# Between two layers: memory products ahead of the transition, and row scaling on VectorE with plain transposes in place of fp32 products with a diagonal

## The chip, the cores and the metric

The kernel runs on one core of a Trainium2 chip. TensorE (PE in the rows, PEld for its weight loads), VectorE (DVE), ScalarE (ACT) and GpSimd (POOL) each run their own queue of instructions in order and wait for each other by semaphores; SyncE (SP) issues the loads from HBM. The metric is the time of one execution on the device in microseconds (us), lower is better.

## The reference, cut to what matters

Two layers run one after the other on 256 tokens of 1024 channels. The first ends in a mixture of experts and a norm with a weight; the second starts with a norm of that result and multiplies it by a wide weight matrix. Beside it, a second input, the memory, is normed and multiplied by its own weights; it depends on nothing of the first layer.

```
x = x + g2 * hier_moe(...)                       # end of the first layer
x = rms_norm(x) * final_norm_w                   # its output
h = rms_norm_2(x, g_mix); proj = h @ w_in        # start of the second
kv_m = rms_norm_2(mem, g_mem) @ w_mem_kv         # (256 x 1024) @ (1024 x 1280)
k_m = rms_norm_2(kv_m[keys], g_k_mem); v_m = kv_m[values]
```

## The kernel before

The 256 tokens stand as two halves of 128 rows. Activations that are multiplied by weights stand transposed, as eight k-tiles of 128 channels by 256 tokens. A float32 product is made of three cheaper ones: each factor is split into a rounded part, hi, and the rest, lo, and the products hi by hi, lo by hi and hi by lo are summed in PSUM. For weights, ScalarE rounds (`whi`, L111) and either GpSimd (L113) or VectorE (L115) subtracts (`wlo`). `unit` makes such a pair for one k-tile of up to 512 columns; four pairs of buffers rotate. Its counter `nunit` with `lo_pool` says who subtracts: every `lo_pool`-th time it is GpSimd. `mm_tok` (L187 to L189) then makes six products per k-tile: hi and lo of the activations with `whi`, and hi with `wlo`, for each half.

`transition` joins the layers. From the four PSUM tiles `moe` it makes w = moe times the norm weight (`tw`, L1207), sums of squares on ScalarE and VectorE, and from them, in some sixteen small VectorE instructions on 128 x 4 values (L1212 to L1218 and `rsqrt`, L126 to L135), two factors per row. One gives the residual `x2` (L1235), the other the second layer's normed input. For that one the kernel makes two 128 x 128 diagonals of the factors, `dm` (`tdm`, L1222), and multiplies each 128 x 128 block of w by its diagonal in float32 (L1229), which scales the rows and transposes them at once. The results are split into `h_hi` on ScalarE (L1114) and `h_lo` on VectorE (L1115), with the gain `g_mix`.

`mem_kv` multiplies the memory (`mh`, `ml`) by its weights in three groups: m = 0, 256 columns of keys, and m = 1 and 2, 512 columns of values each, eight k-tiles per group. In it `lo_pool` is 1, so that GpSimd makes every `wlo`. After the groups the keys are normed (`head_norm_T`: another small VectorE chain, on 128 x 8 values) and transposed (L1161).

`phase_c` is the second layer; its first products take the k-tiles of `h_hi` and `h_lo` against 320 columns of w_in (`tok(320)`). Later stages load 512 columns (2 MB) at a time into three ring buffers, each of which is given back once its k-tiles have been split.

The order of the instructions on each engine is made by a scheduler as the program is built; only SyncE's order is written by hand. Written order counts through `run`: both generators are started, `mem_kv` up to a yield within m = 1, then the rest of `transition`, then the rest of `mem_kv`. `tc.issue_after(i)` puts the instructions that are written in its block behind instruction i on i's engine. Transposes and products of the transition write PSUM tiles of one pool of four banks, which groups m = 0, 1 and 2 use too.

Of the kernel before, what the change touches and what calls it, by code (L numbers as in the profile page):

```python
# [8 lines left out]
F32 = mybir.dt.float32  # L9
# [3 lines left out]
OP = mybir.AluOpType  # L13
# [3 lines left out]
D = 1024  # L17
# [29 lines left out]
class Loader:  # L47
# [31 lines left out]
    def next(self):  # L79
        return self.ready.popleft()[0]  # L80
# [10 lines left out]
class Kern:  # L91
# [1072 lines left out]
    def mem_kv(self, sb, wk):  # L1164
        nc, ld = self.nc, self.ld
        kt = sb.tile([128, 1024], F32, tag="I", name="kmt")[:, 0:512].rearrange("p (t n) -> p t n", t=2)
        self.lo_pool = 1
        for m in range(3):
            w = 512 if m else 256
            p = self.pst2("mm", w)  # L1170
            ch = ld.next()
            v = self.chunk(ch, 8, w)
            for j in range(2):
                k = slice(j * 4, j * 4 + 4)
                self.mm_tok(p, v[:, k], 0, w, self.mh[:, k], self.ml[:, k], start=j == 0, stop=j == 1)
                if m == 1 and j == 0:
                    yield
            ld.give(ch)
            for t in range(2):
                o = self.vm[:, t, 512 * m - 512:512 * m] if m else kt[:, t]  # L1180
                nc.scalar.activation(o, p[t], AF.Copy)
        self.lo_pool = 4
        self.head_norm_T(wk, self.kmT, kt, self.row("g_k_mem"))
# [13 lines left out]
    def transition(self, sb, wk):  # L1197

        nc = self.nc
        jk = sb.tile([128, 2, 512], F32, tag="ck", name="tjk")  # L1200
        jk = [jk[:, 0], jk[:, 1]]
        w = sb.tile([128, 2, D], F32, tag="A", name="tw")
        ss = wk.tile([128, 2, 2, 2], F32, name="tss")
        for h in range(2):
            for t in range(2):
                r = slice(h * 512, h * 512 + 512)
                nc.vector.tensor_tensor(out=w[:, t, r], in0=self.moe[t][h], in1=self.fw[:, r], op=OP.mult)  # L1207
                self.square_sum(jk[0], self.moe[t][h], ss[:, 0, t, h:h + 1])
                sq = self.square_sum if h else self.square_sum_v
                sq(jk[1 - h], w[:, t, r], ss[:, 1, t, h:h + 1])  # L1210
        s = wk.tile([128, 2, 2], F32, name="ts")
        nc.vector.tensor_tensor(out=s, in0=ss[:, :, :, 0], in1=ss[:, :, :, 1], op=OP.add)  # L1212

        v = wk.tile([128, 4], F32, name="tv")
        nc.vector.tensor_scalar(v[:, 0:2], s[:, 0], 1.0 / D, EPS, op0=OP.mult, op1=OP.add)
        e = wk.tile([128, 2], F32, name="te")
        nc.vector.tensor_scalar(e, v[:, 0:2], EPS, None, op0=OP.mult)
        nc.vector.scalar_tensor_tensor(v[:, 2:4], s[:, 1], 1.0 / D, e, op0=OP.mult, op1=OP.add)  # L1218
        r = self.rsqrt(wk, v, 4)
        dm = sb.tile([128, 2048], F32, tag="E", name="tdm")[:, 0:256].rearrange("p (t n) -> p t n", t=2)  # L1220
        for t in range(2):
            nc.vector.tensor_scalar(dm[:, t], self.ident, r[:, 2 + t:3 + t], None, op0=OP.mult)  # L1222
        yield
        for j in range(4):
            p = self.pst("aux")
            for i in range(2):
                for t in range(2):
                    k = 2 * j + i
                    nc.tensor.matmul(p[:, i * 256 + t * 128:i * 256 + t * 128 + 128],  # L1229
                                     w[:, t, k * 128:k * 128 + 128], dm[:, t], start=True, stop=True)  # L1230
            for i in range(2):
                k = 2 * j + i
                self.split_scaled(self.hh[:, k], self.hl[:, k], p[:, i * 256:i * 256 + 256], self.col("g_mix", k))
        for t in range(2):
            nc.vector.tensor_scalar(self.x2[:, t], w[:, t], r[:, t:t + 1], None, op0=OP.mult)  # L1235
# [573 lines left out]
    def run(self, ctx):  # L1809
        nc, tc, a = self.nc, self.tc, self.a  # L1810
# [41 lines left out]
        p = self.xbctx.enter_context(tc.tile_pool(name="r3p", bufs=1))  # L1852
# [3 lines left out]
        with ExitStack() as c:  # L1856
# [15 lines left out]
            sb = cc.enter_context(tc.tile_pool(name="pc", bufs=1, reuse_waits="tile"))  # L1872
# [5 lines left out]
            tr, mk = self.transition(sb, wk), self.mem_kv(sb, wk)  # L1878
            next(tr)
            next(mk)  # L1880
            for part in (tr, mk):
                for _ in part:
                    pass
        self.neg = sb.tile([128, 384], F32, name="neg")
        nc.gpsimd.memset(self.neg, 0.0)
        for o in (0, 256):
# [129 lines left out]
```

## Time and profile before

| what | value |
|---|---|
| median of three runs | 1151.42 us (1149.34 to 1154.03) |
| the profiled execution's own time | 1148.48 us |
| its span, first to last instruction | 1146.8 us |
| TensorE busy | 1058.3 us, 92% of the span |
| VectorE / ScalarE / GpSimd busy | 548.2 / 437.2 / 198.2 us |
| granted TensorE clock, mean | 0.981 |

The times of the rows are microseconds from the span's start. In timeline rows the columns are start, duration, engine, line and operation, output and inputs, shape, and in square brackets how long the engine had been idle and what ended that. A duration runs from start to result; instructions of one engine overlap, so that the pitch between starts is shorter.

### The profile page before, as it was taken

The numbers are of one execution on the slowest core, as the hardware profiler recorded it, in microseconds if no ns is written. First come the engines' busy times: TensorE is split into PE (matmuls) and PEld (weight loads), VectorE is DVE, ScalarE is ACT, GpSimd is POOL, SyncE is SP. The second block draws the span as 40 slices with busy tenths as digits, with TensorE's granted clock in tenths as the row PEclk, the third lists the DMA queues.
The fourth block names the chain that finished last, engine by engine and source line by source line (L and its number), as shares of the span: only waits on it lengthen the run. The fifth ranks groups of instructions, "written<-read, shape, count | busy, mean of one in ns | idle before, by whom it ended". The sixth has DMA issues, their size and how long they took to land.

```text
span 1146.8 us, 18483 instructions
## 1 busy us (share of the span) xinstructions
PE 1058.3 (92%) x6937; PEld 716.6 (62%) x6937; DVE 548.2 (48%) x1345; ACT 437.2 (38%) x982; POOL 198.2 (17%) x189
## 2 busy tenths in 40 slices
PE   4989998999979998987889989998999999999998
PEld 2767777534333431321233678887898888998997
DVE  4498656312121310201221558475796776664664
ACT  3444433211111210101011646565774555655653
POOL 1453112000000000000010732221121132222221
PEclk9999989999989999999999989999999999999999
DMA  9885668599989999999999633552632233554531
GB/s 370 335 349 232 259 260 350 197 421 409 421 336 421 420 417 420 421 422 420 421 421 418 255 141 145 215 184 77 221 108 99 90 148 147 220 185 183 220 147 38
DMA packets 36281, 314.40 MB, mean 274 GB/s; under 512 B 4160, under 2 KB 4672, under 8 KB 5328
## 3 DMA queue, kind: packets, MB, share of 16 engines
q1 hardware_dynamic: 36176, 313.05, 68.1%
q8 instruction: 59, 0.97, 0.3%
q14 instruction: 46, 0.38, 0.1%
HBM read 324.57 MB, written 1.05 MB: 284 GB/s over the span
## 4 chain that ended last, share of the span: by engine, by line
PE 48%; DMA 17%; DVE 4%; ACT 1%; issue 1%; POOL 0%; DVEq 0%; SPq 0%; ACTq 0%
DMA xb<-w 12%; DMA ring<-w 5%; PE mm L176 5%; PE mm L175 5%; PE mm L174 5%; PE pb L937 5%; PE mm L189 4%; PE mm L187 4%; PE mm L188 4%; PE pb L977 3%; PE ff L187 3%; PE ff L188 3%; PE ff L189 3%; PE pb L910 1%; PE aux L1555 1%
## 5 line engine op out<-in xcount | busy, mean ns | idle before, releaser
L111 ACT ACTIVATE whi<-ring 128x512 fp32r<-128x512 f32 (+3 forms) x378 | 228.6, 613 | 196.8 <-PE mm L175 92.6
L113 POOL TENSOR_TENSOR wlo<-ring,whi 128x512 fp32r<-128x512 f32 (+2 forms) x124 | 160.6, 1303 | 499.4 <-ACT whi L111 472.4
L115 DVE TENSOR_TENSOR wlo<-ring,whi 128x512 fp32r<-128x512 f32 (+2 forms) x254 | 177.9, 704 | 139.9 <-ACT whi L111 126.4
L937 PE MATMUL pb<-xb,xT 128*32 128x512 f32 x736 | 134.3, 595 | 9.2 <-DMA xb<-w 9.2
L937 PE MATMUL pb<-ring,xT 128*32 128x512 f32 x672 | 122.5, 595 | 7.0 <-DMA ring<-w 7.0
L963 DVE SCALAR_TENSOR_TENSOR g<-g,pb 128x256 f32<-128x256 f32 x22 | 9.3, 421 | 193.2 <-ACT g L962 193.2
L937 PEld LDWEIGHTS pb<-xb,xT 128*32 128x32 f32 x736 | 34.1, 109 | 87.5 <-issue 60.6
L962 ACT ACTIVATE g<-pb 128x256 f32<-128x256 f32 x22 | 8.4, 383 | 198.2 <-PE pb L937 192.8
L977 PE MATMUL pb<-xb,hT 128*32 128x512 f32 x464 | 79.9, 602 | 2.3 <-DMA xb<-w 1.8
L937 PEld LDWEIGHTS pb<-ring,xT 128*32 128x32 f32 x672 | 30.6, 109 | 72.3 <-issue 51.8
L175 PE MATMUL mm<-h_lo,whi 128*128 128x256 f32 (+1 forms) x264 | 75.3, 285 | 0.0
L176 PE MATMUL mm<-h_hi,wlo 128*128 128x256 f32 (+1 forms) x264 | 75.3, 286 | 0.0
L174 PE MATMUL mm<-h_hi,whi 128*128 128x256 f32 (+1 forms) x264 | 75.2, 285 | 0.0
L113 POOL TENSOR_TENSOR ml<-ring,mh 128x256 fp32r<-128x256 f32 x8 | 5.6, 733 | 400.3 <-DMA xb<-w 400.3
L175 PE MATMUL mm<-xg_lo,whi 128*128 128x256 f32 x256 | 71.2, 280 | 0.0
L174 PE MATMUL mm<-xg_hi,whi 128*128 128x256 f32 x256 | 70.7, 280 | 0.6 <-DVE xg_lo L1115 0.6
L176 PE MATMUL mm<-xg_hi,wlo 128*128 128x256 f32 x256 | 70.9, 279 | 0.0
L187 PE MATMUL mm<-whi,h_hi 128*128 128x512 f32 (+2 forms) x144 | 54.4, 379 | 0.1
L188 PE MATMUL mm<-whi,h_lo 128*128 128x512 f32 (+2 forms) x144 | 53.8, 376 | 0.0
L984 DVE SCALAR_TENSOR_TENSOR Y<-pb,gs,g2row 128x512 f32<-128x512 f32 x22 | 16.5, 750 | 78.0 <-PE pb L977 77.1
L189 PE MATMUL mm<-wlo,h_hi 128*128 128x512 f32 (+2 forms) x144 | 45.6, 379 | 6.1 <-issue 3.8
L176 PEld LDWEIGHTS mm<-h_hi,wlo 128*128 128x128 f32 (+1 forms) x264 | 49.6, 188 | 1.4 <-issue 1.0
(530 smaller groups left out, 2219.5 us busy)
## 6 DMA issues: line engine op xcount, KB each, us to landing
xb<-w SPq DMA_DIRECT2D x110, 1024.0 KB, 15.5
ring<-w SPq DMA_DIRECT2D x82, 1024.0 KB, 13.4
ring<-w_in SPq DMA_DIRECT2D x18, 2048.0 KB, 7.5
ring<-w_ada SPq DMA_DIRECT2D x12, 2048.0 KB, 14.1
ring<-w_up SPq DMA_DIRECT2D x8, 2048.0 KB, 7.3
ring<-w_down SPq DMA_DIRECT2D x8, 2048.0 KB
ring<-w_out SPq DMA_DIRECT2D x2, 2048.0 KB, 11.8
ring<-w_mem_kv SPq DMA_DIRECT2D x2, 2048.0 KB
```

Source lines behind the costliest of these rows:

```text
L111: self.nc.scalar.activation(hi, src, AF.Copy)
L113: self.nc.gpsimd.tensor_tensor(out=lo, in0=src, in1=hi.bitcast(F32), op=OP.subtract)
L115: self.nc.vector.tensor_tensor(out=lo, in0=src, in1=hi.bitcast(F32), op=OP.subtract)
L174: nc.tensor.matmul(out, hv[:, k], xh[:, k0 + k], start=f, stop=False)
L175: nc.tensor.matmul(out, hv[:, k], xl[:, k0 + k], start=False, stop=False)
L176: nc.tensor.matmul(out, lv[:, k], xh[:, k0 + k], start=False, stop=l)
L187: nc.tensor.matmul(out[t], xh[:, k, s], hv[:, 0], start=f, stop=False)
L188: nc.tensor.matmul(out[t], xl[:, k, s], hv[:, 0], start=False, stop=False)
L189: self.last = nc.tensor.matmul(out[t], xh[:, k, s], lv[:, 0], start=False, stop=l)
L937: nc.tensor.matmul(q[r, :], x[:, k, r], w[side[i]][:, h * 512:h * 512 + 512], start=k == 0, stop=k == KT - 1)
L977: nc.tensor.matmul(y[h][r, :], hT[:, f * 128 + i * 32:f * 128 + i * 32 + 32], w[side[i]][:, h * 512:h * 512 + 512], start=f == 0, stop=f == 3)
L984: nc.vector.scalar_tensor_tensor(Y, y[h], gs, self.g2row[:, h * 512:h * 512 + 512], op0=OP.mult, op1=OP.mult)
```

## The change

It does four things. The yield of `mem_kv` moves from the middle of m = 1 to the middle of m = 2, so that when the rest of `transition` is written, all but four k-tiles of the memory's products have been written. The rest of `transition` is put behind the last of those products on TensorE. From m = 1 on `lo_pool` is 2 instead of 1: every other `wlo` of m = 1 and m = 2 is VectorE's. And the diagonals with their float32 products go: VectorE scales the rows of w by the factor in four pieces of 128 x 512 (`ws`, shown as `tws`), and TensorE transposes the sixteen blocks of 128 x 128.

```diff
@@ mem_kv
         for m in range(3):
+            if m:
+                self.lo_pool = 2
...
                 self.mm_tok(p, v[:, k], 0, w, self.mh[:, k], self.ml[:, k], start=j == 0, stop=j == 1)
-                if m == 1 and j == 0:
+                if m == 2 and j == 0:
                     yield
@@ transition
-        dm = sb.tile([128, 2048], F32, tag="E", name="tdm")[:, 0:256].rearrange("p (t n) -> p t n", t=2)
-        for t in range(2):
-            nc.vector.tensor_scalar(dm[:, t], self.ident, r[:, 2 + t:3 + t], None, op0=OP.mult)
+        ws = sb.tile([128, 2, D], F32, tag="E", name="tws")
+        for h in range(2):
+            for t in range(2):
+                c = slice(h * 512, h * 512 + 512)
+                nc.vector.tensor_scalar(ws[:, t, c], w[:, t, c], r[:, 2 + t:3 + t], None, op0=OP.mult)
         yield
...
-                    nc.tensor.matmul(p[:, i * 256 + t * 128:i * 256 + t * 128 + 128],
-                                     w[:, t, k * 128:k * 128 + 128], dm[:, t], start=True, stop=True)
+                    nc.tensor.transpose(p[:, i * 256 + t * 128:i * 256 + t * 128 + 128],
+                                        ws[:, t, k * 128:k * 128 + 128], self.ident)
@@ run
-            for part in (tr, mk):
-                for _ in part:
+            with tc.issue_after(self.last.ins):
+                for _ in tr:
                     pass
+            for _ in mk:
+                pass
```

What this does to the order on TensorE: before, the sixteen products with the diagonals stand behind the last k-tile of m = 1 and in front of all eight of m = 2 (`mm_13574` and `mm_13575` are m = 1, `mm_13697` is m = 2).

```order
L189 MATMUL mm_13574<-wlo_13685,mh 128x512
L189 MATMUL mm_13575<-wlo_13685,mh 128x512
L1229 MATMUL aux_13616<-tdm,tw 128x128
L1229 MATMUL aux_13625<-tdm,tw 128x128
L1229 MATMUL aux_13616<-tdm,tw 128x128 x3
L1229 MATMUL aux_13625<-tdm,tw 128x128 x3
L1229 MATMUL aux_13634<-tdm,tw 128x128 x4
L1229 MATMUL aux_13643<-tdm,tw 128x128 x4
L187 MATMUL mm_13697<-whi_13699,mh 128x512
```

These sixteen (32 instructions) are gone from this place.

After, the first eight transposes stand behind the fourth k-tile of m = 2 (`whi_13693`; the groups' tiles are now `mm_13661` and `mm_13662`), and its last four k-tiles behind them.

```order
L188 MATMUL mm_13662<-whi_13693,ml 128x512
L189 MATMUL mm_13661<-wlo_13694,mh 128x512
L189 MATMUL mm_13662<-wlo_13694,mh 128x512
L1233 MATMUL aux_13703<-ident,tws 128x128 x4
L1233 MATMUL aux_13712<-ident,tws 128x128 x4
L187 MATMUL mm_13661<-whi_13741,mh 128x512
L188 MATMUL mm_13661<-whi_13741,ml 128x512
```

The other eight stand behind all of m = 2 and the first four products of the second layer (`mm_13841`, `mm_13842`).

```order
L187 MATMUL mm_13842<-whi_13843,h_hi 128x320
L188 MATMUL mm_13842<-whi_13843,h_lo 128x320
L1233 MATMUL aux_13721<-ident,tws 128x128 x4
L1233 MATMUL aux_13730<-ident,tws 128x128 x4
L189 MATMUL mm_13841<-wlo_13844,h_hi 128x320
```

On VectorE, before, the end of the transition's small chain stands alone: the last step of `rsqrt`, the diagonals, the residual, and then the first step for the memory's keys.

```order
L133 TENSOR_TENSOR rqt_13475<-rqy_13471 128x4
L134 TENSOR_TENSOR rqt_13475<-rqt_13475,rqw_13473 128x4
L135 SCALAR_TENSOR_TENSOR rqy_13471<-rqt_13475,rqy_13471 128x4
L1222 TENSOR_SCALAR tdm<-ident,rqy_13471 128x128 x2
L1235 TENSOR_SCALAR x_13436<-tw,rqy_13471 128x1024 x2
L120 TENSOR_SCALAR rqv_13792<-hnss_13782 128x8
```

After, two `wlo` stand within that chain (of the seventh k-tile of m = 1, and, here the first row, of the first of m = 2), five steps for the keys lie among its last ones, and the `wlo` of the third k-tile of m = 2 (`wlo_13684`) stands behind the four scalings and half of the residual.

```order
L115 TENSOR_TENSOR wlo_13664<-ring_64,whi_13663 128x512
L133 TENSOR_TENSOR rqt_13475<-rqy_13471 128x4
L134 TENSOR_TENSOR rqt_13475<-rqt_13475,rqw_13473 128x4
L135 SCALAR_TENSOR_TENSOR rqy_13471<-rqt_13475,rqy_13471 128x4
L120 TENSOR_SCALAR rqv_13794<-hnss_13784 128x8
L133 TENSOR_TENSOR rqt_13475<-rqy_13471 128x4
L126 TENSOR_SCALAR rqi_13796<-rqv_13794 128x8
L130 TENSOR_SCALAR rqw_13800<-rqv_13794 128x8
L134 TENSOR_TENSOR rqt_13475<-rqt_13475,rqw_13473 128x4
L128 TENSOR_SCALAR rqy_13798<-rqi_13796 128x8
L135 SCALAR_TENSOR_TENSOR rqy_13471<-rqt_13475,rqy_13471 128x4
L133 TENSOR_TENSOR rqt_13802<-rqy_13798 128x8
```

The steps for the keys are new there. Further on the same queue, where the diagonals and the residual stood, are now the scalings, with a `wlo` between the halves of the residual.

```order
L1226 TENSOR_SCALAR tws<-tw,rqy_13471 128x512 x4
L1239 TENSOR_SCALAR x_13436<-tw,rqy_13471 128x1024
L115 TENSOR_TENSOR wlo_13684<-ring_64,whi_13683 128x512
L1239 TENSOR_SCALAR x_13436<-tw,rqy_13471 128x1024
L134 TENSOR_TENSOR rqt_13802<-rqt_13802,rqw_13800 128x8
```

So the scalings stand behind more of VectorE's queue than the diagonals did, and the `wlo` of a product on TensorE stands behind the scalings. On ScalarE two roundings stand between the third and the last of the transition's square sums instead of three; on GpSimd eight of the sixteen subtractions of m = 1 and m = 2 are gone; SyncE's order is the same.

## Rows read from the trace of the kernel before

**Rows 1.** The page's first line: the span.

```profile
span 1146.8 us, 18483 instructions
```

**Rows 2.** Stretches: length, busy time per engine (count), granted clock, DMA share, GB/s.

```profile
647.00:658.50 11.50, 10.54 (x47) 8.25 (x45) 5.57 (x8) 9.90 (x35) 11.50 (x10) 1.00 0.36 125
658.50:663.80 5.30, 0.00 (x0) 0.00 (x0) 4.95 (x13) 1.24 (x3) 3.35 (x3) 0.90 0.87 354
663.80:670.10 6.30, 6.28 (x31) 6.28 (x32) 3.95 (x15) 2.07 (x5) 0.00 (x0) 0.54 0.01 3
670.10:1146.80 476.70, 465.50 (x2890) 412.38 (x2888) 309.74 (x725) 277.73 (x632) 107.78 (x84) 1.00 0.41 151
```

**Rows 3.** Timeline of TensorE around the products with the diagonals.

```profile
656.98 0.39 PE L187 MATMUL mm<-whi,mh 128*128 128x512 f32 x1
...
657.88 0.61 PE L189 MATMUL mm<-wlo,mh 128*128 128x512 f32 x2
663.82 1.01 PE L1229 MATMUL aux<-tdm,tw 128*128 128x128 f32 x3 [5.32 <-DVE tdm L1222]
...
670.16 0.47 PE L187 MATMUL mm<-whi,mh 128*128 128x512 f32 x1
```

**Rows 4.** Instructions on the diagonals' tile: min/median/max in ns, first and last start.

```profile
L1229 PE MATMUL aux<-tdm,tw x32: 275/421/579, 663.8 to 670.1; 128*128 128x128 f32 x32
```

**Rows 5.** Timeline of VectorE, the transition's small chain.

```profile
652.86 0.36 DVE L1212 TENSOR_TENSOR ts<-tss 128x4 f32<-128x4 f32 x1 [5.80 <-ACT tjk L1107]
653.25 1.22 DVE L1215 TENSOR_SCALAR tv<-ts 128x2 f32<-128x2 f32 x1
...
660.69 1.18 DVE L133 TENSOR_TENSOR rqt<-rqy 128x4 f32<-128x4 f32 x1
661.90 0.16 DVE L134 TENSOR_TENSOR rqt<-rqt,rqw 128x4 f32<-128x4 f32 x1
...
663.48 0.48 DVE L1222 TENSOR_SCALAR tdm<-ident,rqy 128x128 f32<-128x128 f32 x2
663.87 1.41 DVE L1235 TENSOR_SCALAR x<-tw,rqy 128x1024 f32<-128x1024 f32 x2
```

**Rows 6.** Timeline of GpSimd over the same time.

```profile
646.44 15.41 POOL L113 TENSOR_TENSOR wlo<-ring,whi 128x512 fp32r<-128x512 f32 x12
```

**Rows 7.** Timeline of VectorE later: two square sums of one shape.

```profile
689.94 1.35 DVE L1110 SCALAR_TENSOR_TENSOR jv<-ck 128x256 f32<-128x256 f32 x1 [0.83 <-ACT ck L1284]
...
691.67 0.42 DVE L1110 SCALAR_TENSOR_TENSOR jv<-ck 128x256 f32<-128x256 f32 x1
```

**Rows 8.** Timeline of GpSimd over the first of these.

```profile
689.72 1.30 POOL L113 TENSOR_TENSOR wlo<-ring,whi 128x512 fp32r<-128x512 f32 x1 [3.12 <-ACT whi L111]
```

**Rows 9.** Groups by shape, 640 to 672 us: count, busy, mean ns, idle before.

```profile
L111 ACT ACTIVATE whi<-ring 128x512 fp32r<-128x512 f32 x12 | 7.4, 628 | 2.3 <-PE mm L188 1.6 <-issue 0.5 <-POOL wlo L113 0.2
...
L189 PE MATMUL mm<-wlo,mh 128*128 128x512 f32 x18 | 5.8, 396 | 1.0 <-POOL wlo L113 1.0
...
L1115 DVE SCALAR_TENSOR_TENSOR h_lo<-aux,pk,h_hi 128x256 fp32r<-128x256 f32 x8 | 3.8, 482 | 2.4 <-ACT h_hi L1114 2.3
...
L1114 ACT ACTIVATE h_hi<-aux,pk 128x256 fp32r<-128x256 f32 x8 | 3.5, 471 | 8.7 <-PE aux L1229 8.5 <-DVE h_lo L1115 0.2
```

**Rows 10.** Groups by shape over the whole span: VectorE's subtraction.

```profile
L115 DVE TENSOR_TENSOR wlo<-ring,whi 128x512 fp32r<-128x512 f32 x236 | 169.5, 721 | 130.5 <-ACT whi L111 122.4 <-PE mm L189 4.7 <-DVEq L1465 2.4
```

**Rows 11.** Timeline of TensorE later: ten plain transposes and what follows them.

```profile
829.92 1.25 PE L1192 MATMUL aux<-ident,qn 128*128 128x128 f32 x10
830.92 0.36 PE L174 MATMUL mm<-h_hi,whi 128*128 128x256 f32 x1
```

**Rows 12.** Timeline of SyncE: loads of w_in.

```profile
679.74 7.21 SPq L104 DMA_DIRECT2D ring<-w_in  x2
```

**Rows 13.** Timeline of TensorE: the first product with the second chunk.

```profile
705.14 0.40 PE L187 MATMUL mm<-whi,h_hi 128*128 128x512 f32 x1
```

**Rows 14.** Timeline of TensorE: its longest wait for VectorE in the second layer.

```profile
711.34 0.73 PE L189 MATMUL mm<-wlo,h_hi 128*128 128x512 f32 x2 [2.23 <-DVE wlo L115]
```

## The prediction

> **What bounds the kernel now.** The change touches one place, so the stretch between the layers was read first, by windows [rows 2]. From 647.0 to 658.5 us TensorE is busy for 10.54 of 11.50 us. Then it does nothing for 5.3 us while DVE works for 4.95, and for the next 6.3 us it is busy at a granted clock of 0.54, about the lower of its two levels, 1.2 GHz. From 670.1 to the end it is busy for 465.50 of 476.70 us, and the DMA engines for 0.41 of it: behind this place TensorE sets the time, and what it wins here should reach the end.
>
> The timeline of TensorE says what the two pieces are [rows 3]. The last product of m = 1 ends at 657.88 + 0.61 = 658.49. The idle 5.32 us after it end on DVE's `tdm`, the diagonals; then come the 32 records of the products with diagonals [rows 4], and the first product of m = 2 starts at 670.16. So 670.16 − 658.49 = 11.67 us lie between two groups that depend on nothing of the first layer: 5.32 of waiting and 6.35 of products.
>
> The timelines of DVE and GpSimd say why `tdm` is late [rows 5, 6]. DVE's chain of sixteen small instructions starts with `ts` at 652.86 (released by ScalarE's last square sum) and reaches `tdm` at 663.48. While GpSimd subtracts without a gap, twelve in 15.41 us (1.28 each) from 646.44 to 661.85, a DVE instruction on four columns takes 1.2 us, one for each GpSimd instruction; from 661.90 on eight of them fit into 663.48 − 661.90 = 1.58 us, 0.198 each. Some 7 us of the chain's 10.6 are thus waiting for GpSimd.
>
> **The change part by part.** *Removed:* the whole 11.67 us from TensorE's order, if what fills the hole is ready in time.
>
> *Transposes added.* Ten plain transposes run from 829.92 to the next product at 830.92, 0.10 us each [rows 11]; sixteen are **+1.6 us**. At the lower clock they could be twice that, 3.2; I take 1.6, as work runs up to them and the clock was 1.00 while it did [rows 2].
>
> *Moved: when the scalings must be ready.* Four products of 512 columns start between 656.98 and 657.88, 0.225 us each, and a k-tile has six: 1.35 us [rows 3]. With four k-tiles of m = 2 put in, the first transpose is due at 658.49 + 4 × 1.35 = 663.89.
>
> *When they are ready.* `ts` starts when ScalarE ends its last square sum; one rounding fewer stands ahead of it, 0.63 us [rows 9], of which I take 0.55. DVE's work from there, without GpSimd's hindrance: sixteen steps of 0.198 = 3.16; two subtractions of 0.72 [rows 10] = 1.44; five steps for the keys, 0.99; four scalings of 128 x 512. For these the near rows are two `tdm` of 128 columns in 0.48 and two halves of `x` of 1024 in 1.41 [rows 5], 0.24 and 0.70 each, between them 0.44; four are 1.75. Together 7.34.
>
> GpSimd, which now makes every other `wlo`, runs one of 1.28 us for each two k-tiles (2.7 us), three or four while the chain runs. Each may hold DVE for between 0 and 1.28 us, so 0 to 5.1 in all. I take 2.2, somewhat under half, since GpSimd now stands still for half of the time. The scalings end at 652.86 − 0.55 + 7.34 + 2.2 = 661.85, two microseconds ahead of their due time: no wait of the transposes.
>
> The split of the subtractions is where a rule speaks against the change. First the rows: a square sum of 128 x 256 on DVE, started 0.22 us after a subtraction on GpSimd, lasts 1.35 us and ends with it, at 691.29 against 691.02; the same shape takes 0.42 without one beside it [rows 7, 8]. The Trainium skill, SBUF — State Buffer, section "SBUF: two separate sides", states that VectorE and GpSimd share a read/write port pair under an exclusive lock held for the whole instruction, so that whichever of the two comes late is fully blocked. The trace agrees. By that rule alone a `wlo` split over both engines would not run in parallel at all, and each DVE instruction of the chain could again cost a whole GpSimd instruction; that is the second rival below.
>
> *Moved: a `wlo` behind the scalings.* The third k-tile of m = 2 has its `wlo` on DVE, behind the scalings and half of the residual. It is ready at 661.85 + 0.70 + 0.72 = 663.27. It is due when TensorE has done two k-tiles and four products of the third: 658.49 + 2 × 1.35 + 4 × 0.225 = 662.09. **+1.2 us** of waiting, the value I take. With no hindrance by GpSimd it is 661.07 and nothing is waited for; with all of it, 666.2, that is 4.1, and with the full 0.63 or none of it 4.0 to 4.6; I carry 0 to 4.4. A wait of 1.2 moves the transposes by as much, to 665.1, which only adds to their slack.
>
> *The first `wlo` of m = 1.* TensorE waits 1.0 us for GpSimd's `wlo` there [rows 9]. DVE may now make one in 0.72 instead of 1.28, but from m = 0 GpSimd is still behind. I take **0**, with a bound of 1.0 us gained.
>
> *Evacuation of the transposes.* Each k-tile needs 0.47 on ScalarE and 0.48 on DVE [rows 9]. Eight transposes end near 665.9; four k-tiles are split by 665.9 + 0.47 + 4 × 0.48 = 668.3, and with DVE's two remaining subtractions by 669.7. The last four k-tiles of m = 2, 5.4 us, cover that until 671.3. The other eight transposes are split while TensorE does the products of the first four k-tiles with w_in. **0**; if the cover failed, 1.28 for each GpSimd instruction in the way. Before, TensorE likewise had m = 2 behind the transition, so no cover of that kind is lost.
>
> *The loads.* SyncE's order is unchanged. The chunk of w_in issued at 679.74 takes 7.2 us and is first used at 705.14 [rows 12, 13], 18 us of slack, and all that frees its buffer moves earlier with TensorE. **0**.
>
> The sum: −11.67 + 1.6 + 1.2 = −8.87, say **−8.9 us**. The profiled execution, of whose time all but 1.7 us is its span [rows 1], comes to 1148.48 − 8.9 = 1139.6. It lies 2.94 under the median of the runs, so the median becomes 1151.42 − 8.9 = **1142.5**. TensorE's busy time should fall by about 4.7 and the rest is idle time removed.
>
> **The rivals.**
>
> *A, slower: GpSimd holds DVE at full price.* If every one of the six GpSimd subtractions left beside the chain delays DVE by 1.28 us, the chain bears 7.7 instead of 2.2: the scalings end at 667.35, the third `wlo` at 668.8. TensorE then waits 668.8 − 662.1 = 6.7 us, and, idle that long, may be slowed as it was after 5.3 idle us: 6.28 × (1 − 0.54) = 2.9 us lost [rows 2]. If the waiting falls into two such stretches, each with its slowdown, the cost is 6.7 + 5.8 = 12.5 against 11.67 − 1.6 = 10.07 won. The same hold then falls on the splits of the transposed rows, for the last two subtractions of m = 2 and the first for w_in, 3 × 1.28 = 3.8 that a late TensorE has no cover for: 16.3 − 10.07 = 6.2 slower, 1157.6. It decides from a third `wlo` later than 662.1 + 10.07 − 5.8 = 666.4, where the waits with their two spells alone use up the gain. For it speaks that each of the chain's first steps before took a whole GpSimd instruction; against it that GpSimd now waits for ScalarE's roundings in between, and the first subtractions are done before the chain starts.
>
> *B: the lock eats most of it.* By the trace's own 1.28 per step, four GpSimd instructions fully paid make the wait 4.4, and one spell at the lower clock costs 2.9: 7.3 of the 10.07 are lost, the gain is 2.8, the median 1148.6. The rule of the Trainium skill named above, taken strictly, leads here.
>
> *C: the gain is given back later.* At 711.34 TensorE waits 2.23 us for a DVE `wlo` [rows 14]; DVE and ScalarE carry the norms of the second layer there. If TensorE arrives 8.9 earlier and their work does not move with it, the wait could grow by about 5, and the median is 1147. Against it: that work starts from products that themselves come 8.9 earlier.
>
> That the change does not do what it says is excluded: the order on TensorE shows the sixteen products gone and the transposes where the diff puts them.
>
> **How the numbers follow.** Forecast 0.77, A 0.05, B 0.10, C 0.08. Own bounds of the forecast: with no wait and the 1.0 us won, 10.07 + 1.0 = 11.1, that is 1140.3; with 4.4 of waiting, 10.07 − 4.4 = 5.7, that is 1145.7. The runs of before lie between 2.1 below and 2.6 above their median; with that the range goes from 1138.0 to 1148.0, which takes in C and most of B's neighbourhood. About 0.5% is what a measurement of this kernel can tell from no change, here 5.8 us: faster means under 1145.7. The forecast gives 0.77 of that with its worst end on the border, and a part of C adds 0.02: faster 0.79. B and the rest of C make 0.16 the same; A makes 0.05 slower. The range leaves out A and the part of B above 1148.
>
> **What would show it.** Right: between the last product of m = 1 and the first transpose TensorE is never idle for more than about 2 us; the granted clock there stays at 1.0; sixteen transposes of about 0.10 stand where 6.35 us of products stood; GpSimd has eight subtractions fewer and DVE eight more; the last scaling ends by about 662 to 664; the idle time that is left ends on DVE's third `wlo` of m = 2. Wrong: a wait of several microseconds for that `wlo`, DVE steps of 1.2 us throughout the chain, a stretch at a clock near 0.5 around the transposes, or a wait near 700 us that has grown by more than 3.

## The result: 1136.3 us, and the profile of the changed kernel

The changed kernel takes 1136.3 us in the median of four runs (1133.88 to 1139.55), beside 1151.9 for the kernel before. The ratio is 0.9871 (95% interval 0.9856 to 0.9887), that is 13 to 16.6 us faster. The forecast was 1142.5 with a range from 1138.0 to 1148.0: the direction was right, but the gain is some 1.7 times the 8.9 us that were worked out, and it lies outside the range.

The page of the profiled execution (1137.99 us) begins like this. TensorE has 16 products and 16 weight loads fewer than before, GpSimd eight subtractions fewer:

```profile
span 1136.2 us, 18447 instructions
## 1 busy us (share of the span) xinstructions
PE 1056.9 (93%) x6921; PEld 710.8 (63%) x6921; DVE 554.6 (49%) x1355; ACT 436.1 (38%) x982; POOL 189.4 (17%) x181
```

**Between the layers.** The timeline of TensorE answers to [rows 3]. The two memory groups now run on without a gap to the third k-tile of m = 2, whose `wlo` TensorE waits for; the first eight transposes take 669.16 − 668.37 = 0.79 us:

```profile
660.76 1.07 PE L189 MATMUL mm<-wlo,mh 128*128 128x512 f32 x4
...
666.41 0.72 PE L189 MATMUL mm<-wlo,mh 128*128 128x512 f32 x2 [2.32 <-DVE wlo L115]
...
668.37 1.03 PE L1233 MATMUL aux<-ident,tws 128*128 128x128 f32 x8
669.16 0.47 PE L187 MATMUL mm<-whi,mh 128*128 128x512 f32 x1
```

The windows of the same stretch (length, busy time by engine, granted clock, DMA share, GB/s) answer to [rows 2]. The clock is 1.00 throughout, behind the wait too:

```profile
661.00:663.90 2.90, 2.90 (x14) 2.24 (x12) 2.90 (x8) 2.19 (x4) 1.76 (x2) 1.00 0.99 416
663.90:666.41 2.51, 0.19 (x1) 0.00 (x0) 2.51 (x4) 0.00 (x0) 0.92 (x1) 1.00 0.08 34
666.41:669.20 2.79, 2.79 (x17) 2.39 (x17) 2.62 (x10) 1.46 (x3) 0.33 (x1) 1.00 0.00 0
```

The timeline of VectorE answers to [rows 5], the one of GpSimd, below it, to [rows 6]. VectorE's small steps take 0.16 us where GpSimd is idle. Where GpSimd starts a subtraction while VectorE is at work, one VectorE instruction is held until that is over: the `tv` of 1.25, the `wlo` of 1.80 in place of 0.68, and two of the four scalings, which together take 3.81.

```profile
654.72 0.52 DVE L1214 TENSOR_TENSOR ts<-tss 128x4 f32<-128x4 f32 x1 [0.80 <-ACT tjk L1107]
...
656.16 1.25 DVE L1220 SCALAR_TENSOR_TENSOR tv<-ts,te 128x2 f32<-128x2 f32 x1
...
658.36 1.80 DVE L115 TENSOR_TENSOR wlo<-ring,whi 128x512 fp32r<-128x512 f32 x1
...
661.29 3.81 DVE L1226 TENSOR_SCALAR tws<-tw,rqy 128x512 f32<-128x512 f32 x4
665.02 0.74 DVE L1239 TENSOR_SCALAR x<-tw,rqy 128x1024 f32<-128x1024 f32 x1
665.68 0.68 DVE L115 TENSOR_TENSOR wlo<-ring,whi 128x512 fp32r<-128x512 f32 x1
```

```profile
656.04 1.36 POOL L113 TENSOR_TENSOR wlo<-ring,whi 128x512 fp32r<-128x512 f32 x1 [0.83 <-ACT whi L111]
658.32 1.29 POOL L113 TENSOR_TENSOR wlo<-ring,whi 128x512 fp32r<-128x512 f32 x1 [0.92 <-ACT whi L111]
661.52 1.40 POOL L113 TENSOR_TENSOR wlo<-ring,whi 128x512 fp32r<-128x512 f32 x1 [1.91 <-PE mm L189]
663.54 1.27 POOL L113 TENSOR_TENSOR wlo<-ring,whi 128x512 fp32r<-128x512 f32 x1 [0.62 <-ACT whi L111]
```

**Behind it.** The other part of the gain is seen only when the two traces are laid beside each other from a product that both have to another. The last products of the experts and the next group of eight products that both have stand, in the timeline of TensorE, of before at

```profile
642.62 0.62 PE L991 MATMUL moe<-Yl,S 128*128 128x512 f32 x2
...
696.52 1.99 PE L1347 MATMUL aux<-w,w 16*128 16x256 f32 x8
```

and of after at

```profile
645.49 0.62 PE L991 MATMUL moe<-Yl,S 128*128 128x512 f32 x2
...
691.08 1.99 PE L1351 MATMUL aux<-w,w 16*128 16x256 f32 x8
```

That is 53.90 us before and 45.59 after: 8.3 us won at the transition. From there to the span's end it is 450.28 before and 445.12 after: another 5.2 us, where the change touches nothing. (Ahead of the transition the profiled execution of after is 2.9 us later than that of before. No kernel here changes anything there, and yet the last product of the experts starts between 642.0 and 647.0 us in the 14 traces of this document, so traces are compared from that product on.)

What TensorE waited for in the second half, in all, by line, with times and the longest: first of the kernel before, then of after.

```profile
PE aux L1229 <- DVE tdm L1222: 5.3, 1, 5.3
PE mm L189 <- issue: 3.8, 1, 3.8
PE mm L189 <- DVE wlo L115: 2.2, 1, 2.2
PE mm L189 <- POOL wlo L113: 1.0, 1, 1.0
```

```profile
PE mm L189 <- DVE wlo L115: 4.0, 2, 2.3
PE mm L175 <- DVE xg_lo L1115: 0.9, 1, 0.9
PE mm L174 <- DVE xg_lo L1115: 0.6, 1, 0.6
PE mm L188 <- issue: 0.2, 1, 0.2
```

A wait of 3.8 us that nothing in the profile ends ("issue") has become one of 0.2. In the timeline of the kernel before it stands at 795.21, behind `tc.If(wide > 0)` (L1465), a branch over a body that is not run:

```profile
791.04 0.39 PE L188 MATMUL mm<-whi,h_lo 128*128 128x512 f32 x1
795.21 0.61 PE L189 MATMUL mm<-wlo,h_hi 128*128 128x512 f32 x2 [3.78 <-issue]
```

and the windows show half the clock behind it, another 3.80 × (1 − 0.59) = 1.6 us:

```profile
791.40:795.20 3.80, 0.03 (x1) 0.00 (x0) 2.24 (x10) 2.01 (x9) 0.00 (x0) 1.00 0.38 151
795.20:799.00 3.80, 3.79 (x11) 3.00 (x11) 0.69 (x1) 0.89 (x3) 0.64 (x1) 0.59 0.02 4
```

Of the 3.8 us, 0.2 are left: 3.8 − 0.2 + 1.6 = 5.2 us are the second part. TensorE's busy time tells the same: from the last product of the experts on it is 486.1 us before and 479.7 after, 6.4 less, of which 6.28 − 1.6 = 4.7 are the products with the diagonals less the transposes, and the rest is that slow stretch. (Over the whole span it is only 1.4 less, as the execution of after is busier ahead of that product.) The experiments ask first why that wait went, and then what each part of the change did at the transition.

### The profile page after: what moved, and what is told of

It is laid out like the page before. It is cut to its first block, busy times and chain, and to the rows that moved or that the text cites. A ratio compares the mean times of both kernels' runs of the same rounds, so it can differ in the third digit from the quotient of the medians.

```text
span 1136.2 us, 18447 instructions
## 1 busy us (share of the span) xinstructions
PE 1056.9 (93%) x6921; PEld 710.8 (63%) x6921; DVE 554.6 (49%) x1355; ACT 436.1 (38%) x982; POOL 189.4 (17%) x181
## 3 DMA queue, kind: packets, MB, share of 16 engines
HBM read 324.57 MB, written 1.05 MB: 287 GB/s over the span
## 5 line engine op out<-in xcount | busy, mean ns | idle before, releaser
L115 DVE TENSOR_TENSOR wlo<-ring,whi 128x512 fp32r<-128x512 f32 (+3 forms) x262 | 185.2, 710 | 130.5 <-ACT whi L111 118.7
L113 POOL TENSOR_TENSOR wlo<-ring,whi 128x512 fp32r<-128x512 f32 (+2 forms) x116 | 152.5, 1318 | 494.0 <-ACT whi L111 468.6
L977 PE MATMUL pb<-xb,hT 128*32 128x512 f32 x464 | 82.4, 629 | 1.7 <-DMA xb<-w 1.2
L977 PE MATMUL pb<-ring,hT 128*32 128x512 f32 x240 | 50.0, 632 | 3.7 <-ACT hT L968 1.9
L175 PEld LDWEIGHTS mm<-h_lo,whi 128*128 128x128 f32 (+1 forms) x264 | 49.7, 188 | 1.2 <-issue 1.0
```

The source lines that it names most:

```text
L113: self.nc.gpsimd.tensor_tensor(out=lo, in0=src, in1=hi.bitcast(F32), op=OP.subtract)
L115: self.nc.vector.tensor_tensor(out=lo, in0=src, in1=hi.bitcast(F32), op=OP.subtract)
L175: nc.tensor.matmul(out, hv[:, k], xl[:, k0 + k], start=False, stop=False)
L977: nc.tensor.matmul(y[h][r, :], hT[:, f * 128 + i * 32:f * 128 + i * 32 + 32], w[side[i]][:, h * 512:h * 512 + 512], start=f == 0, stop=f == 3)
```

## The experiments

**The theory of the wait behind the branch.** Code comes by DMA on queues of its own. The page of the kernel before lists on one of them 59 packets of 0.97 MB, 16 KB each. It names no engine for the queue; it is taken for TensorE's, as that makes one packet for some 240 of TensorE's instructions. In the second half of the trace such a packet comes about every 20 us, but three come within 11 us behind the branch: the code is fetched anew there. Just then, at 785.94, a 2 MB load of w_in is issued. Theory P: TensorE ran out of code because the second block behind the branch came late, and how much code the first block still holds there depends on where the branch's target lies in its block. The change takes 34 instructions (16 products, 16 weight loads, 2 semaphore instructions) out of TensorE's code ahead of that place, so the target lies 34 instructions earlier in its block, and the block lasts that much longer. Rival Q: the times of that execution, by chance.

*before_again* is the kernel before, unchanged.

> The kernel before, unchanged, profiled a second time. It tells whether the wait of TensorE behind the branch (the conditional at L1465 of the kernel before; 3.78 us, ended by nothing that the profile shows) belongs to the program or to one execution. Theory P (place in the code: TensorE runs out of instructions because its next block of code comes late): the wait stands at the same instruction again, 3 to 4.5 us long, with a stretch at the lower clock behind it. Rival Q (chance): it is gone or stands elsewhere.

It took 1152.1 us, and in its timeline the wait stands at the same product:

```profile
797.83 0.63 PE L189 MATMUL mm<-wlo,h_hi 128*128 128x512 f32 x2 [3.85 <-issue]
```

The wait belongs to the program. *after_shift* and *before_shift* move nothing but the code's place, by instructions in the body that is not run:

```diff
@@ gla_general, called inside the conditional
         p = self.pst("aux")
+        if h == 0:
+            for _ in range(17):    # 111 in before_shift
+                nc.tensor.transpose(p[:, 0:128], self.ident, self.ident)
```

> The kernel after, with 17 transposes put into the body of the conditional, which is not run: it adds no work, but the code behind the conditional lies some 34 TensorE instructions further on, about where it lies in the kernel before. Theory P: the wait behind the branch, 3.8 us, is back at about the 21st product behind it, with the lower clock for some 4 us after it (another 1.5 us): 5 us slower than the kernel after, near 1141 us, ratio to before about 0.991. Rival Q (the wait depends on when the transfers come, not on the code's place): no wait there, 1136 us as the kernel after, ratio 0.987.

> The kernel before, with 111 transposes put into the body of the conditional, which is not run: the code behind the conditional then lies, counted modulo the 256 instructions of one 16 KB block, where it lies in the kernel after. Theory P: the wait of 3.8 us behind the branch is gone with nothing else changed: about 5 us faster than before, near 1147 us, ratio 0.9955. Rival Q: 1152 us, ratio 1.000, the wait stays.

after_shift took 1140.73 us (ratio to before 0.9902, 0.9887 to 0.9917), 4.4 above the kernel after. Its timeline and windows have the wait back, and the lower clock with it:

```profile
783.18 0.40 PE L189 MATMUL mm<-wlo,h_hi 128*128 128x512 f32 x1
787.15 0.79 PE L189 MATMUL mm<-wlo,h_hi 128*128 128x512 f32 x1 [3.57 <-issue]
```

```profile
783.60:787.10 3.50, 0.00 (x0) 0.00 (x0) 1.31 (x9) 1.10 (x5) 0.00 (x0) 0.98 0.31 122
787.15:789.00 1.85, 1.84 (x4) 1.49 (x5) 0.69 (x1) 0.00 (x0) 0.00 (x0) 0.50 0.04 9
789.00:791.00 2.00, 2.00 (x7) 1.58 (x6) 0.00 (x0) 0.89 (x3) 0.36 (x1) 0.66 0.00 0
```

before_shift took 1144.63 us (ratio 0.9944, 0.9931 to 0.9958), and TensorE runs through that place:

```profile
792.08 0.62 PE L189 MATMUL mm<-wlo,h_hi 128*128 128x512 f32 x2
792.53 0.39 PE L187 MATMUL mm<-whi,h_hi 128*128 128x512 f32 x1
```

Q is out: the same work with the code elsewhere has the wait or has it not, in both kernels. The size by the traces is 4.0 us for the one (laid beside the kernel after from the last products of the experts to the end) and 5.3 for the other. By the medians it is 4.4 and 7.5, by the ratios to before 3.6 and 6.5, the latter with an interval from 4.8 to 7.9.

The traces also show how P works, counted from the branch. In before and before_again TensorE stops ahead of the 44th of its instructions behind the branch. In the kernel after, the 0.2 us that are left stand ahead of the 78th, 34 instructions further on:

```profile
789.27 0.39 PE L188 MATMUL mm<-whi,h_lo 128*128 128x512 f32 x1 [0.23 <-issue]
```

The second block is no sooner there: its packet starts 6.1 us behind the first in after and 5.9 in before_shift, beside 5.8 in before, and TensorE goes on 9.6 us behind the branch in after, 9.3 in before. What the code's place changes is how much work the first block still holds until then.

*before_small* leaves out seven eighths of that load and asks whether the load makes the block late.

```diff
-            for w in widths:
-                ld.add(self.load(a[n][:, off:off + 8 * w], 8 * w))
+            for i, w in enumerate(widths):
+                short = 8 if widths == W2S[6:] and i == 4 else 1
+                ld.add(self.load(a[n][:, off:off + 8 * w // short], 8 * w // short))
```

> The kernel before, with one load cut to an eighth (256 KB of 2 MB): the chunk of w_in that is issued as TensorE takes the branch. The products with it run on old data, so the output is not the reference's. Theory P with collision (the block of code is late because its transfer stands behind the load's packets): the code packet that came at 792.8 us comes some microseconds earlier, the wait of 3.8 us is gone, about 5 us faster, near 1147 us. Rival: the block is asked for late whatever the load does (its time hangs on how far TensorE has come): the wait stays, 1152 us.

It took 1147.96 us (0.9961, 0.9946 to 0.9976). In before the DMA engines are almost full with the load while the second block is due, as the DMA view of 788.6 to 792.0 us shows (queue, packets, MB, share of 16 engines); the block's packet starts at 792.8, 5.8 us behind the first one:

```profile
q1 hardware_dynamic: 85, 1.39, 95.5%
```

With the short load it starts 3.3 us behind the first, and of the wait 0.98 us is left, at the same product (the profile puts it to a VectorE instruction; but it stands ahead of the 44th instruction again, and TensorE goes on 1.2 us after the end of the block's packet, beside 1.4 in before):

```profile
795.88 0.63 PE L189 MATMUL mm<-wlo,h_hi 128*128 128x512 f32 x2 [0.98 <-DVE jv L1111]
```

So the load is a part of the cause, some 2.5 us of the block's lateness. The other 3.3 us are there with hardly any load; whether the block is asked for that late or takes that long is not shown. Every kernel below has its code behind the branch within two instructions of where the kernel after has it; the base for them is before_shift with 1144.6 us.

**The transition, part by part.** Theory S: it was GpSimd that held VectorE's chain, and the split of the `wlo` frees it. Rival O: the order does it, by giving TensorE work in the meantime. Rival T: the transposes do. *split_alone* takes only the split into the kernel before, *order_no_split* takes it out of the kernel after, *order_diagonals* puts the fp32 products back into the kernel after. Not shown in the cut below: split_alone and order_diagonals have the 111 transposes of before_shift in the body that is not run.

```diff
@@ split_alone: mem_kv of the kernel before
         for m in range(3):
+            if m:
+                self.lo_pool = 2
@@ order_no_split: mem_kv of the kernel after
-            if m:
-                self.lo_pool = 2
@@ order_diagonals: transition of the kernel after
-                nc.vector.tensor_scalar(ws[:, t, c], w[:, t, c], r[:, 2 + t:3 + t], None, op0=OP.mult)
+            nc.vector.tensor_scalar(dm[:, t], self.ident, r[:, 2 + t:3 + t], None, op0=OP.mult)
...
-                    nc.tensor.transpose(..., ws[:, t, k * 128:k * 128 + 128], self.ident)
+                    nc.tensor.matmul(..., w[:, t, k * 128:k * 128 + 128], dm[:, t], start=True, stop=True)
```

> The kernel before with one part of the change, every other wlo of m = 1 and 2 on VectorE; the fp32 products with the diagonals stay where they were, behind m = 1. Its code behind the branch is put where the kernel after has it, so that the wait behind the branch is out of the comparison (base: the shifted kernel before, 1144.6 us). Theory S (the hole in TensorE's order was GpSimd holding VectorE's chain; the split alone removes most of it): the diagonals are ready some 15.6 us behind the last product of the experts as in the kernel after, m = 1 ends 1 us earlier; the wait of 5.3 us falls to about 1, the wait of 1.0 for GpSimd goes, the products run at the full clock (3.6 instead of 6.35): about 8 us faster, 1136.6 us. Rival O (the order is what matters, products of the memory in the hole): the wait stays near 4 us and the low clock with it, 1143 us.

> The kernel after with lo_pool left at 1, so that GpSimd makes all sixteen wlo of m = 1 and 2; order and transposes as after. Theory S: GpSimd is busy without a gap until some 20 us behind the last product of the experts, each step of VectorE's chain takes 1.2 us, the scalings come 5 to 7 us too late, TensorE waits at the transposes and runs at the lower clock behind them: 7 to 9 us slower than the kernel after, 1143 to 1145 us. Rival O: the order alone does it, 1136 to 1138 us.

> The kernel after with the diagonals and the sixteen fp32 products in place of the scalings and transposes; order and split as after, code behind the branch where the kernel after has it. Theory (by the terms): the products cost 32 x 0.112 = 3.6 us at the full clock instead of 1.6, and VectorE's two diagonals of 0.24 in place of four scalings (3.8 with GpSimd's holds) let the third wlo of m = 2 come in time, so that the wait of 2.3 goes: 0.3 us faster to 0.5 slower than the kernel after, 1136 to 1137 us. Rival T (the transposes are the gain): 3 us or more slower, 1139 or above.

The last column is from the traces: the time from the experts' last product to the span's end. It is of one execution each; for two executions of the kernel before it is 504.2 and 505.8.

| kernel | median, us | ratio to before (95%) | wait at the transition | trace, us |
|---|---|---|---|---|
| before_shift (base) | 1144.63 | 0.9944 (0.9931 to 0.9958) | 1.0 and 5.3 | 498.9 |
| split_alone | 1141.74 | 0.9914 (0.9894 to 0.9935) | 2.2 | 496.0 |
| order_no_split | 1143.51 | 0.9936 (0.9920 to 0.9953) | 1.0 and 4.2 | 496.4 |
| order_diagonals | 1138.71 | 0.9895 (0.9879 to 0.9912) | 1.8 | 492.7 |
| after | 1136.3 | 0.9871 (0.9856 to 0.9887) | 2.3 | 490.7 |

Split alone gives 2.9 of the 8 us that theory S gave it. The order with the transposes but without the split gives 1.1, which the intervals do not tell from nothing; its trace has 2.5. Neither does it alone: order and split together give 5.9, and all three parts 8.3. In split_alone the chain is sooner, the diagonals come 16.9 us behind the experts' last product instead of 20.9, but they are due as soon as m = 1 ends; 2.2 us of wait stay, and the windows show that this was enough for the lower clock over most of the products:

```profile
659.25:661.40 2.15, 0.00 (x0) 0.00 (x0) 2.15 (x11) 1.24 (x3) 1.27 (x1) 0.99 1.00 420
661.47:664.50 3.03, 3.03 (x14) 3.03 (x15) 2.55 (x8) 0.47 (x1) 0.00 (x0) 0.50 0.50 206
664.50:667.00 2.50, 2.50 (x21) 2.46 (x21) 2.11 (x9) 1.79 (x5) 0.00 (x0) 0.95 0.00 0
```

In order_no_split GpSimd is busy for the whole of the first window (16.30 of 16.30 us) and nearly every step of VectorE's chain takes 1.2 us as before. The scalings come 4.2 us late although they are due four k-tiles later, and again half the clock follows. This half of theory S held, and it is rival A of the prediction in small:

```profile
652.00:668.30 16.30, 15.64 (x68) 12.69 (x68) 10.73 (x11) 12.75 (x40) 16.30 (x14) 1.00 0.52 199
668.40:672.50 4.10, 0.00 (x0) 0.00 (x0) 3.89 (x8) 0.24 (x1) 2.88 (x3) 0.78 0.12 28
672.56:678.00 5.44, 5.44 (x18) 4.52 (x19) 5.07 (x21) 0.95 (x2) 0.00 (x0) 0.54 0.87 352
```

order_diagonals comes 2.4 us behind the kernel after by the medians (the intervals overlap) and 2.0 by the traces, between what the terms gave (0.5 at most) and what rival T gave (3 or more). So the transposes are a part of the gain, some 2 of the 8 us, and not the bulk. The price of the products is as the terms had it: the sixteen run at the full clock, 32 records 0.112 us apart, 3.6 us instead of 1.6. What was not foreseen is that the wait did not go; the third `wlo` still comes 1.8 us late behind diagonals, both halves of the residual and the holds, and here the wait is followed by the lower clock (3.64 × 0.47 = 1.7 us), which the longer one in the kernel after is not:

```profile
662.53:664.30 1.77, 0.01 (x1) 0.00 (x0) 1.77 (x4) 0.00 (x0) 1.15 (x1) 1.00 0.05 19
664.36:668.00 3.64, 3.64 (x10) 2.86 (x11) 3.43 (x13) 1.26 (x2) 0.00 (x0) 0.53 0.00 0
```

**What is left of the waits.** *wlo_first* puts the `wlo` of the third k-tile ahead of the scalings in VectorE's queue, and *residual_last* the residual behind the last `wlo` of m = 2 as well; *scale_on_scalar* has two of the scalings on ScalarE besides. *no_gpsimd_m2* leaves the order alone and has VectorE make all `wlo` of m = 2, *no_gpsimd_m1_m2* those of m = 1 too. The cut leaves out where residual_last and scale_on_scalar write the residual and resume `transition` in `run`.

```diff
@@ wlo_first, residual_last, scale_on_scalar: transition (self.lo: VectorE's last wlo)
-                nc.vector.tensor_scalar(ws[:, t, c], ...)
+                with self.tc.issue_after(self.lo.ins):    # wlo_first: and x2 behind the scalings
+                    nc.vector.tensor_scalar(ws[:, t, c], ...)
+                # scale_on_scalar: nc.scalar.activation(..., scale=r[:, 2 + t:3 + t]) for t = 1
@@ no_gpsimd_m2 (no_gpsimd_m1_m2: 999 for both): mem_kv
-                self.lo_pool = 2
+                self.lo_pool = 2 if m == 1 else 999
```

> The kernel after with one change of VectorE's order: the wlo of the third k-tile of m = 2 ahead of the four scalings, and the residual behind them. If the wait of 2.3 us in the kernel after comes from that wlo's place in VectorE's queue alone, it goes, and the first eight transposes, which need only the first two scalings, still find them ready: 2.3 us faster than the kernel after, 1134 us. Rival: the wait moves to the transposes (scalings late by 1.4 to 2 us), no gain, 1136 us.

> The kernel after with the wlo of the third k-tile of m = 2 ahead of the scalings and the residual (two times 1024 columns on VectorE) behind the last wlo of m = 2. In the run wlo_first the wait of 2.3 us had moved to the wlo of the fifth k-tile, 1.5 us, which stood behind scalings and residual. Theory (VectorE's queue order is all that is left of the waits): no wait of TensorE above 0.5 us between m = 1 and the second layer, granted clock 1.0 throughout; 1 to 1.5 us faster than wlo_first, 2.3 faster than the kernel after: 1134 us against 1150.7 for before, ratio 0.985 to 0.986. Rival: VectorE is simply full there and the wait moves on to h_lo or to a later wlo: as wlo_first, 0.987.

> The run residual_last with two of the four scalings on ScalarE, at about 0.6 us each. Theory: VectorE's two held scalings (1.5 us each with a hold) leave its queue, but the roundings of the next k-tiles on ScalarE come 1.2 us later, and with them GpSimd's wlo of the fourth k-tile: no wait above 1 us either way, the time within 1 us of residual_last, 1134 to 1135 us. Rival (VectorE is the limit there): another 1 us or more faster, 1133 us or less.

> The kernel after with all eight wlo of m = 2 on VectorE, so that GpSimd stands still while the scalings run. Theory (GpSimd holds each VectorE instruction that meets a subtraction of its own, by about 1.05 us): the four scalings take 1.9 to 2.0 us in place of 3.81, and no instruction of the chain beside m = 2 lasts above its bare time; what VectorE gains there, about 2 us, it pays with four more wlo of 0.69: the time stays within 1.5 us of the kernel after, 1135 to 1138 us. Rival (the scalings are slow by themselves at 512 columns): they still take 3.5 us or more, and the time rises by 2 to 3 us.

> The kernel after with all sixteen wlo of m = 1 and m = 2 on VectorE; GpSimd makes none beside the transition. In the run no_gpsimd_m2 the four scalings fell to 1.67 us and no wait was left between m = 1 and the second layer, 1132.5 us. Theory (a hold of 1.05 us costs VectorE more than the 0.69 us of making that wlo itself): no VectorE instruction beside the memory's products lasts above its bare time and TensorE waits nowhere there: 1132 to 1133 us, ratio 0.984 to 0.985. Rival (VectorE becomes the bound: its chain starts behind seven wlo of m = 1): a wait of 1 us or more for a wlo or for the scalings is back, 1134 us or above.

| kernel | median, us | ratio to before (95%) | waits at the transition | trace, us |
|---|---|---|---|---|
| after | 1136.3 | 0.9871 (0.9856 to 0.9887) | 2.3 | 490.7 |
| wlo_first | 1135.13 | 0.9869 (0.9853 to 0.9886) | 1.5, for the fifth `wlo` | 489.8 |
| residual_last | 1133.59 | 0.9855 (0.9838 to 0.9871) | 0.4 | 487.9 |
| scale_on_scalar | 1134.3 | 0.9862 (0.9846 to 0.9878) | none over 0.3 | 487.6 |
| no_gpsimd_m2 | 1132.46 | 0.9846 (0.9829 to 0.9862) | none over 0.3 | 486.6 |
| no_gpsimd_m1_m2 | 1132.63 | 0.9841 (0.9827 to 0.9854) | none over 0.3 | 486.6 |

wlo_first moved the wait rather than removing it: TensorE found the transposes ready, and waited 1.5 us for the next `wlo` behind scalings and residual. residual_last removed that too, as expected. For single steps the intervals overlap; the waits are read from the traces.

no_gpsimd_m2 went better than either theory had it, and it settles the hold. The groups of VectorE around the transition (busy time, mean ns of one) have the four scalings in residual_last, where GpSimd subtracts beside them, at

```profile
L1228 DVE TENSOR_SCALAR tws<-tw,rqy 128x512 f32<-128x512 f32 x4 | 3.7, 994 | 0.0
```

and in no_gpsimd_m2, where it does not, at

```profile
L1226 DVE TENSOR_SCALAR tws<-tw,rqy 128x512 f32<-128x512 f32 x4 | 1.7, 480 | 0.0
```

In the kernel after, from which no_gpsimd_m2 differs by its `wlo` alone, they take the 3.81 us shown above. So they are not slow by themselves. In this window of no_gpsimd_m2 TensorE is busy for all of 16.00 us, with the clock at 1.00, and VectorE, which makes all subtractions of m = 2, still has 1.5 us to spare:

```profile
655.00:671.00 16.00, 16.00 (x84) 13.71 (x83) 14.50 (x46) 10.38 (x21) 0.87 (x1) 1.00 0.67 257
```

GpSimd's help cost more than it gave: a `wlo` of 0.69 us that VectorE does not make is paid with a hold of about 1.05. A better order on VectorE hides most of that: residual_last, where GpSimd still helps, is within 1.2 us of no_gpsimd_m2, and their intervals overlap. Taking m = 1 from GpSimd as well gains nothing more that can be measured. Both versions beat both kernels: they lie 3 to 4 us below the changed one by the ratios, the medians and the traces, though the interval of no_gpsimd_m2 still overlaps that of the kernel after by a little.

## Why the prediction was right and wrong

**The hole and what fills it: right.** The sum was −8.9 us for the transition. The terms as the trace has them: −11.67 removed, +1.6 for the transposes (0.79 for eight), +2.3 for the third `wlo`, −1.0 for the first `wlo` of m = 1, together −8.8, and the traces laid beside each other say −8.3. Like for like, with the code in the same place, before_shift to after is 8.3 us by the medians and 8.2 by the traces; before to after_shift is 11.4 (9.6 to 13.0 by the interval) and 9.5 by the traces (11.2 from before_again).

**The first `wlo` of m = 1:** taken as 0 with a bound of 1.0 won; the whole 1.0 was won.

**GpSimd's hold: under-sized.** "I take 2.2, somewhat under half." Four subtractions ran beside the chain and the scalings, and each held VectorE for nearly its whole length: 1.25 − 0.17 = 1.1 at `tv`, 1.80 − 0.68 = 1.1 at the `wlo`, 3.81 − 1.67 = 2.1 at the scalings, 4.3 of the 5.1 that the bound allowed. What GpSimd's idle half of the time was thought to spare does not follow: VectorE's queue never paused, so each subtraction met an instruction. The Trainium skill, SBUF — State Buffer, section "SBUF: two separate sides", has whichever starts first keep the shared ports for its whole instruction and the other fully blocked, if VectorE's instruction runs in a two-port mode or has two inputs in SBUF and GpSimd's reads SBUF; the trace agrees, with holds of 1.05 to 1.1 us against subtractions of 1.27 to 1.40. The `tv` and the `wlo` held here have two such inputs; the mode of the scalings no run shows.

**The wait for the third `wlo`:** 1.2 was taken, 2.3 measured, within the bound of 4.4. When the `wlo` is ready was forecast almost to the point, by errors that nearly cancel: 663.27 − 642.62 = 20.65 us behind the last experts' product, against 665.68 + 0.68 − 645.49 = 20.87. The larger hold was mostly offset, as `ts` started about 1 us sooner (654.72 − 645.49 = 9.23 behind that product against 652.86 − 642.62 = 10.24), where 0.55 was taken, and as the rest of the chain took 1.4 us less than reckoned. What made the wait longer is that TensorE came sooner: 666.41 − 2.32 − 645.49 = 18.60 us behind that product, against 662.09 − 642.62 = 19.47. So the 1.0 us won at the first `wlo` of m = 1 was nearly all lost again here, and that the two together came out near the forecast is in part luck.

**The evacuation and the loads at 0: right.** TensorE waits neither for `h_hi` or `h_lo` nor for a load at this place. The wait of 2.23 in [rows 14] did not grow, as rival C had it; in after it is 1.7. Rivals A and B did not come, but order_no_split shows A's mechanism: a wait of 4.2 with the lower clock behind it.

**The step that failed:** "behind this place TensorE sets the time, and what it wins here should reach the end." What was won did reach the end; what failed is that the stretch behind was taken to stay otherwise as it was. The row that this rests on, the last of [rows 2], has 465.50 busy of 476.70 us; a third of the idle 11.2 was the wait for code behind the branch. It was read as fixed, while it depends on where the code lies, and the change takes 34 TensorE instructions out ahead of it. No term of the sum stood for that, and the bounds of the range therefore held only the transition. With −5.2 for it the sum would have been −14.1: 1137.3, against 1136.3. The experiments show that the code's place alone moves 4.0 us in the one kernel and 5.3 in the other by the traces, so a third of the gain is an accident of this program: before_shift has it from 222 instructions that are never run.

## What to carry to other kernels

When a change adds or removes instructions, look up every wait in the trace that nothing ends ("issue") and that lies behind a branch or a big load: it may come or go by the code's place alone. To compare two versions, put that place equal, by instructions in a body that is not run. And count a second engine's help against what it holds up: where VectorE and GpSimd both work without pause, a piece of work given to GpSimd can cost VectorE more than doing it.

## What was not expected of the hardware

The code of an engine travels through the same DMA engines as the data, here in blocks of 16 KB. Behind a branch a 2 MB load that is issued at the same moment made the second block some 2.5 us later. With the code where the kernel before has it, TensorE stopped there for 3.6 to 3.9 us in three traces out of three; with it 34 instructions further up, the block was as late, and the stop was 0.2 us or none.

The clock falls behind waits much shorter than the 5.3 us of before, but not behind all. It was 0.50 over 3.03 us behind a wait of 2.2 (split_alone), 0.53 over 3.64 behind 1.8 (order_diagonals), 0.50 and 0.66 over 3.85 behind 3.6 (after_shift), and 1.00 behind 2.3 (after) and behind 1.5 (wlo_first). What tells the 1.8 from the 2.3 these runs don't show.
